# Gate projections of a hybrid decoder block: weight sums without a negation, one of four made by an accumulating load

## The chip, the cores and the metric

The kernel runs on one core of a Trainium2 chip. The metric is the device time of one execution in microseconds (us). The kernel before took 425.77 us in the median of three runs (425.74 to 426.47). Durations below come from one further execution that was recorded by the hardware profiler.

The core has a matrix engine (TensorE, "PE" in the profile), a vector engine (VectorE, "DVE"), an activation engine (ScalarE, "ACT"), a general engine (GpSimd, "POOL") and a queue engine that only issues transfers (SyncE, "SP"). TensorE writes its results to PSUM banks. ScalarE, GpSimd and SP issue transfers (DMAs). Every engine works through its own queue of instructions in order and waits on semaphores for the others.

## The reference

The input x has 512 rows and 1024 columns. It is normalised, multiplied with one wide weight matrix, and the product is cut into the inputs of two attention branches and of two gates:

```
h = rms_norm(x, norm_g);  proj = h @ w_in
fq, fk, fv, fz, mq, mk, mv, mz, ga, gb, fl = split_cols(proj, IN_SPLITS)
y_fox  = fox_attention(...)  * silu(fz)      # 8 heads of 64, with a forget gate
y_moba = moba_attention(...) * silu(mz)      # 8 heads of 64, block-sparse
merged = sigmoid(ga + b_gate[0]) * (y_fox @ w_fox) + sigmoid(gb + b_gate[1]) * (y_moba @ w_moba)
x = x + merged @ w_out
```

The change concerns `ga` and `gb`: two products of h (512 x 1024) with a 1024 x 1024 slice of `w_in` each, followed by a bias and a sigmoid.

## The kernel before

All numbers are float32. Each matmul operand is split into a high part and the rest (`hi` and `lo`), and a product is made of three matmuls: high by high, low by high, high by low. A weight block of 128 x 1024 elements is split by one ScalarE instruction (line 141, `hi`) and one VectorE subtraction (line 143, `lo`). There are four buffers each for `hi` and `lo` and four (`wr`) for raw weights.

The work is staged: loads, normalisation and the first projections; four attention groups (fox a, fox b, moba a, moba b) with the remaining projections laid between their steps; the gates; the output projection. The gates come in four groups, GA0, GA1, GB0 and GB1. Between GB0 and GB1, and after GB1, stand the output products of the moba branch (`wm0` to `wm3`).

Each gate group computes 256 columns out of each half of its gate with a Strassen–Winograd scheme: the activations are cut into blocks A11, A12, A21, A22 (halves of the rows and of the 1024 columns of h), the weights into W11, W12, W21, W22, and seven products take the place of eight. Four of the seven use sums of activation blocks, S1 to S4, and four use sums of weight blocks, T1 to T4.

The activation sums are made once, in `make_sums`, during the first attention group: for each of four pairs of h blocks four VectorE instructions of 128 x 256 elements (line 274), then a split; the parts go to DRAM, and GpSimd's queue loads them back as the gates begin (line 291, eight transfers of 512 KB).

In each group, `group` has

- four loads of 512 KB on SP's queue (line 728), in the order W11, W12, W22, W21;
- seven preparations (`prep`). Each splits one block or sum; ahead of the second, fourth and sixth stand subtractions of 128 x 1024 elements on VectorE (line 723), four in all;
- seven products (`product`, lines 759, 761 and 762) of 24 matmuls each, 256 columns wide, in the order of `PRODUCTS`: A11, S3, A12, S2, S1, A22, S4. They accumulate in three PSUM banks;
- after each product an `evac` step: ScalarE keeps a bank's partial result in SBUF (line 769), or VectorE adds a kept one to a bank (line 772); `finish` applies the sigmoid on ScalarE (lines 802, 804, 805).

`pump` orders loads and preparations around the products: ahead of a unit of TensorE work it queues preparations up to three ahead of it, and a load as soon as the preparation that last reads the buffer it will take has been queued. Each load carries the number of its block's last preparation for that. A planner then sets the order in each engine's queue from its own estimates of durations, under the dependencies of the data.

GpSimd's queue holds, in the moba groups, powers and products for the norms (lines 343, 345), the products of line 670, then the loads of line 291, and, beside the first gate group, two instructions that spread the last head pair's reciprocal row sums (line 663). TensorE transposes those (line 666). In the output stage it issues accumulating loads (`minus`, line 897): ScalarE negates a weight block in place and GpSimd's transfer adds another one from DRAM to it.

Of the kernel before, what the change touches and what calls it, by code (L numbers as in the profile page):

```python
# [9 lines left out]
AF = mybir.ActivationFunctionType  # L10
OP = mybir.AluOpType
# [3 lines left out]
S = 512  # L15
# [4 lines left out]
CW = 256  # L20
# [9 lines left out]
def fox_moba_kernel(ctx: ExitStack, tc, xT, x, w_in, w_fl, w_fox, w_moba, w_out, cst, rope, out):  # L30


    nc = tc.nc
    V, A, G, T = nc.vector, nc.scalar, nc.gpsimd, nc.tensor
# [14 lines left out]
    def t2(tag, bufs, name, shape=(P, 512), dt=F32):  # L49
        pool = stage["pool"] if tag in ("qs", "pt", "pc", "ys") else sb  # L50
        return pool.tile(list(shape), dt, name=name, tag=tag, bufs=bufs)

    def pst(tag, bufs, name):
        return ps.tile([P, 512], F32, name=name, tag=tag, bufs=bufs)
# [36 lines left out]
    def col(c, n=1):  # L91
        return cs[:, c:c + n]
# [45 lines left out]
    def split(src, n, name, half=False):  # L138
        hi = sb.tile([P, 4, 264], F32R, name=f"wh_{name}", tag="wh", bufs=4)
        lo = sb.tile([P, 4, 264], F32R, name=f"wl_{name}", tag="wl", bufs=4)  # L140
        A.activation(hi[:, :, 0:n], src, AF.Copy)  # L141
        for eng, q in ((V, slice(0, 2)), (G, slice(2, 4))) if half else ((V, slice(0, 4)),):
            eng.tensor_tensor(out=lo[:, q, 0:n], in0=src[:, q], in1=hi[:, q, 0:n].bitcast(F32), op=OP.subtract)  # L143
        return hi, lo
# [27 lines left out]
    COLS = {}  # L172
# [87 lines left out]
    HT = S // 2  # L260
# [4 lines left out]
    def make_sums(k):  # L265
        def tl(tag, dt=F32):
            return t2("y", 15, f"sum_{tag}", dt=dt)
        a, b = XT[k], XT[k + 4]
        out = []
        f0, f1 = tl("sf"), tl("sf")  # L270
        s3, s2, s1, s4 = f0[:, 0:HT], f0[:, HT:S], f1[:, 0:HT], f1[:, HT:S]
        for o, x, y, op in ((s3, a[:, 0:HT], a[:, HT:S], OP.subtract), (s1, a[:, HT:S], b[:, HT:S], OP.add),
                            (s2, s1, a[:, 0:HT], OP.subtract), (s4, b[:, 0:HT], s2, OP.subtract)):
            V.tensor_tensor(out=o, in0=x, in1=y, op=op)
        for i, f in enumerate((f0, f1)):
            hl = [tl("sh", F32R), tl("sl", F32R)]
            A.activation(hl[0], f, AF.Copy)
            V.tensor_tensor(out=hl[1], in0=f, in1=hl[0].bitcast(F32), op=OP.subtract)
            out.extend((d[2 * i:2 * i + 2, :, k, :].rearrange("s p t -> p s t"),
                        t.bitcast(F32).rearrange("p (s t) -> p s t", t=HT)) for d, t in zip(S_dram, hl))  # L280

        def store():
            for d, t in out:
                A.dma_start(out=d, in_=t)
        return store
# [7 lines left out]
    def left(what, k):  # L293
        if what[0] == "S":
            return [x[:, k] for x in SB[S_AT[what]]]
        t, kk = int(what[1]) - 1, 4 * (int(what[2]) - 1) + k
        return [x[:, kk, t * HT:(t + 1) * HT] for x in (Gh, Gl)]
# [411 lines left out]

    PRODUCTS = (("A11", 1), ("S3", 3), ("A12", 2), ("S2", 1), ("S1", 1), ("A22", 3), ("S4", 1))
    groups = {}

    def group(name):
        ga, i = name[1] == "A", int(name[2])
        wa, wb = (f"g{'a' if ga else 'b'}{i}", f"g{'a' if ga else 'b'}{i + 2}")
        st = {}
        R, B = {}, {}
        base = len(preps)  # L720

        def sub(o, a, b):
            V.tensor_tensor(out=o, in0=a, in1=b, op=OP.subtract)

        def load(key, nm, hf):
            def go():
                R[key] = sb.tile([P, 4, CW], F32, name=f"wr_{nm}{hf}", tag="wr", bufs=WR)
                nc.sync.dma_start(out=R[key], in_=w_in[COLS[nm] // CW, :, 4 * hf:4 * hf + 4, :])
            return go

        def prep(n):

            def go():
                if n == 1:
                    sub(R["11"], R["12"], R["11"])
                    sub(R["12"], R["22"], R["12"])
                elif n == 3:
                    sub(R["12"], R["22"], R["11"])
                elif n == 5:
                    sub(R["21"], R["21"], R["12"])  # L740
                key = ("11", "12", "21", "12", "11", "21", "22")[n]
                B[n] = split(R[key], CW, f"{name}{n}")
            return go
        for key, nm, hf, last in (("11", wa, 0, 4), ("12", wb, 0, 5), ("22", wb, 1, 6), ("21", wa, 1, 5)):
            loads.append((load(key, nm, hf), base + last))
        preps.extend(prep(n) for n in range(7))

        def product(n):
            what, b = PRODUCTS[n]
            if n < 3:  # L750
                st[b] = pst(("pj", "tp", "tp")[b - 1], (2, 3, 3)[b - 1], f"pb{b}_{name}")
            p = st[b]
            hi, lo = B[n]
            for c in range(2):
                o = p[:, c * HT:(c + 1) * HT]
                cc = slice(c * P, (c + 1) * P)
                for k in range(4):
                    lh, ll = left(what, k)
                    T.matmul(o, hi[:, k, cc], lh, start=(n < 3 and c == 0 and k == 0), stop=False,  # L759
                             skip_group_check=True)  # L760
                    T.matmul(o, hi[:, k, cc], ll, start=False, stop=False, skip_group_check=True)  # L761
                    T.matmul(o, lo[:, k, cc], lh, start=False, stop=(k == 3), skip_group_check=True)  # L762

        def two(a):
            return a.rearrange("p (c t) -> p c t", t=HT)

        def keep(n, b):
            st["e", n] = stage["pool"].tile([P, S], F32, name=f"e{n}_{name}", tag="e", bufs=3)
            A.activation(st["e", n], st[b], AF.Copy)

        def add(u, half, n, b):
            V.tensor_tensor(out=u[:, :, half * HT:(half + 1) * HT], in0=two(st[b]), in1=two(st["e", n]), op=OP.add)

        def evac(n):
            if n == 0:
                if ga or i == 0:
                    u = [sb.tile([P, 2, S], F32, name=f"u{name}{q}", tag="qk", bufs=4) for q in range(2)]
                else:
                    v4 = sb.tile([P, 4, S], F32, name=f"u{name}", tag="v", bufs=2)
                    u = [v4[:, 0:2, :], v4[:, 2:4, :]]  # L780
                st["u"] = u
                keep(1, 1)
            elif n == 1:
                keep(3, 3)
            elif n == 2:
                add(st["u"][0], 0, 1, 2)
            elif n == 3:
                keep(2, 1)
            elif n == 4:
                add(st["u"][1], 1, 3, 1)  # L790
            elif n == 5:
                add(st["u"][0], 1, 2, 3)
                finish(0)
            else:
                finish(1)

        def finish(q):
            u, j0 = st["u"][q], 2 * i + 4 * q
            bg = C_BG + (0 if ga else 8)
            for c in range(2):  # L800
                if q == 0:
                    A.activation(u[:, c, :], u[:, c, :], AF.Sigmoid, bias=col(bg + j0 + c))
                else:
                    A.activation(u[:, c, 0:HT], two(st[1])[:, c, :], AF.Sigmoid, bias=col(bg + j0 + c))
                    A.activation(u[:, c, HT:S], u[:, c, HT:S], AF.Sigmoid, bias=col(bg + j0 + c))
            if ga:
                f = FS[j0 // 2]
                V.tensor_tensor(out=f, in0=u, in1=f, op=OP.mult)
            else:
                SG[j0 // 2] = u  # L810

        def unit(n):
            def go():
                product(n)
                evac(n)
            return go
        groups[name] = [unit(n) for n in range(7)]
# [295 lines left out]
    prep, product, evac, sub, result = (groups[k] for k in ("prep", "product", "evac", "sub", "out"))  # L1113
# [115 lines left out]
```

## Time and profile before

| what | value |
|---|---|
| median of the runs | 425.77 us (425.74 to 426.47) |
| the profiled execution | 425.43 us |
| its span on the core | 423.4 us |
| TensorE matmuls, busy | 417.7 us |
| VectorE, busy | 326.8 us |
| ScalarE, busy | 269.5 us |
| GpSimd, busy | 106.3 us |
| moved by DMA | 58.21 MB |

The span runs from the first to the last record of the core; 425.43 - 423.4 = 2.0 us lie around it. In the profile's rows, a group shows line, engine, operation, output and inputs, count, then busy time in us and mean duration in ns, and after the last bar the idle time of the engine before these instructions with what ended it. A timeline row shows start and duration in us. "L723" is line 723 of the kernel. The row of a line or a tile shows the shortest, median and longest duration in ns and the first and last start.

### The profile page before, as it was taken

The numbers are of one execution on the slowest core, as the hardware profiler recorded it, in microseconds if no ns is written. First come the engines' busy times: TensorE is split into PE (matmuls) and PEld (weight loads), VectorE is DVE, ScalarE is ACT, GpSimd is POOL, SyncE is SP. The second block draws the span as 40 slices with busy tenths as digits, with TensorE's granted clock in tenths as the row PEclk, the third lists the DMA queues.
The fourth block names the chain that finished last, engine by engine and source line by source line (L and its number), as shares of the span: only waits on it lengthen the run. The fifth ranks groups of instructions, "written<-read, shape, count | busy, mean of one in ns | idle before, by whom it ended". The sixth has DMA issues, their size and how long they took to land.

```text
span 423.4 us, 7713 instructions
## 1 busy us (share of the span) xinstructions
PE 417.7 (99%) x2913; PEld 388.9 (92%) x2913; DVE 326.8 (77%) x570; ACT 269.5 (64%) x515; POOL 106.3 (25%) x120
## 2 busy tenths in 40 slices
PE   8999999999999999999999999999999999999996
PEld 6998899999999998899998888899999989988885
DVE  4679977899967768578676787767979698689883
ACT  4986327778767767567656686756656535686450
POOL 1065730225136550016660202140000000022330
PEclk9999999999999999999999999999999999999999
DMA  7973334666263323314123222473042603696484
GB/s 242 396 257 112 100 101 127 183 198 211 77 209 108 100 78 125 82 45 124 31 96 114 88 74 82 154 279 110 31 170 66 233 2 121 206 253 116 100 142 157
DMA packets 25621, 58.21 MB, mean 137 GB/s; under 512 B 3064, under 2 KB 7856, under 8 KB 25584
## 3 DMA queue, kind: packets, MB, share of 16 engines
q1 hardware_dynamic: 13392, 38.11, 27.7%
q10 hardware_dynamic: 8800, 11.21, 8.7%
q0 software_dynamic: 3392, 8.39, 8.5%
q8 instruction: 23, 0.38, 0.3%
q14 instruction: 14, 0.11, 0.1%
HBM read 48.11 MB, written 6.32 MB: 129 GB/s over the span
## 4 chain that ended last, share of the span: by engine, by line
PE 97%; DMA 1%; SPq 0%; DVE 0%; issue 0%; ACT 0%
PE pb_GB L762 3%; PE pb_GA L762 3%; PE pb_GB L759 3%; PE pb_GA L759 3%; PE pb_GB L761 3%; PE pb_GA L761 3%; PE po L950 3%; PE po L949 3%; PE po L948 3%; PE lg L565 2%; PE pv L620 2%; PE pv L619 2%; PE lg L564 2%; PE pf L690 2%; PE pf L689 2%; PE pm L690 2%
## 5 line engine op out<-in xcount | busy, mean ns | idle before, releaser
L343 POOL TENSOR_TENSOR ff<-ss,mh 128x8 f32<-128x8 f32 x16 | 32.0, 2005 | 71.0 <-DVE ss L341 63.2
L567 DVE CUSTOM_DVE_ANT_0 p<-lg,mask 128x128 f32<-128x128 f32 (+1 forms) x64 | 30.6, 488 | 15.7 <-PE lg L565 15.3
L569 ACT ACTIVATE p<-p,negm 128x128 f32<-128x128 f32 (+1 forms) x64 | 35.6, 557 | 10.0 <-DVE negm L567 9.7
L897 POOL DMA_DIRECT2D wr_o<-in_w_out_dram x4 | 4.9, 1293 | 95.4 <-DMA wr_o<-in_w_out_dram 87.2
L143 DVE TENSOR_TENSOR wl_GA<-wr_ga,wh_GA 128x1024 fp32r<-128x1024 f32 x14 | 16.9, 1223 | 7.6 <-ACT wh_GA L141 5.8
L141 ACT ACTIVATE wh_GA<-wr_ga 128x1024 fp32r<-128x1024 f32 x14 | 14.6, 1059 | 9.9 <-PE pb_GA L761 4.9
L141 ACT ACTIVATE wh_GB<-wr_gb 128x1024 fp32r<-128x1024 f32 x14 | 14.6, 1059 | 9.5 <-PE pm L689 3.5
L564 PE MATMUL lg<-KH,QS 128*128 128x128 f32 (+1 forms) x64 | 20.3, 327 | 0.0
L910 ACT ACTIVATE wh_o<-wr_o 128x1024 fp32r<-128x1024 f32 x14 | 14.8, 1060 | 8.2 <-PE pb_GB L761 2.8
L911 DVE TENSOR_TENSOR wl_o<-wr_o,wh_o 128x1024 fp32r<-128x1024 f32 x14 | 17.0, 1221 | 3.8 <-ACT wh_o L910 3.8
L143 DVE TENSOR_TENSOR wl_GB<-wr_gb,wh_GB 128x1024 fp32r<-128x1024 f32 x14 | 16.9, 1222 | 3.5 <-ACT wh_GB L141 3.5
L645 DVE TENSOR_TENSOR ypair<-pv,ysh 64x512 f32<-64x512 f32 x16 | 11.0, 687 | 5.8 <-ACT ysh L644 5.5
L337 DVE TENSOR_REDUCE ss<-sq 128x8 f32<-128x512 f32 x16 | 10.9, 679 | 4.6 <-ACT sq L336 4.5
L538 DVE SCALAR_TENSOR_TENSOR QS<-p_qT,cs,QS 64x512 fp32r<-64x512 f32 x16 | 12.0, 750 | 2.4 <-ACT QS L537 2.0
L759 PE MATMUL pb_GA<-Gh,wh_GA 128*128 128x256 f32 x48 | 13.6, 282 | 0.0
L761 PE MATMUL pb_GA<-Gl,wh_GA 128*128 128x256 f32 x48 | 13.5, 281 | 0.0
L762 PE MATMUL pb_GA<-Gh,wl_GA 128*128 128x256 f32 x48 | 13.5, 281 | 0.0
L762 PE MATMUL pb_GB<-Gh,wl_GB 128*128 128x256 f32 x48 | 13.5, 281 | 0.0
L761 PE MATMUL pb_GB<-Gl,wh_GB 128*128 128x256 f32 x48 | 13.4, 281 | 0.0
L759 PE MATMUL pb_GB<-Gh,wh_GB 128*128 128x256 f32 x48 | 13.3, 281 | 0.0
L542 DVE SCALAR_TENSOR_TENSOR KL<-p_kT,cs,KH 64x512 fp32r<-64x512 f32 x16 | 12.0, 749 | 1.3 <-ACT KH L540 0.8
L537 ACT ACTIVATE QS<-p_qT,cs 64x512 fp32r<-64x512 f32 x16 | 10.9, 680 | 3.3 <-DVE QS L538 2.2
(459 smaller groups left out, 1792.8 us busy)
## 6 DMA issues: line engine op xcount, KB each, us to landing
wr_ga<-in_w_in_dram SPq DMA_DIRECT2D x8, 512.0 KB
wr_gb<-in_w_in_dram SPq DMA_DIRECT2D x8, 512.0 KB, 5.1
wr_o<-in_w_out_dram SPq DMA_DIRECT2D x8, 512.0 KB, 12.6
xt<-in_xT_dram SPq DMA_DIRECT2D x8, 256.0 KB, 6.9
x<-in_x_dram SPq DMA_DIRECT2D x8, 256.0 KB, 6.0
KH<-KH ACTq DMA_DIRECT2D x16, 128.0 KB, 4.8
s_dramh<-sum_sh ACTq DMA_DIRECT2D x8, 256.0 KB, 5.5
s_draml<-sum_sl ACTq DMA_DIRECT2D x8, 256.0 KB, 2.5
```

The costliest lines, as they stand in the source:

```text
L141: A.activation(hi[:, :, 0:n], src, AF.Copy)
L143: eng.tensor_tensor(out=lo[:, q, 0:n], in0=src[:, q], in1=hi[:, q, 0:n].bitcast(F32), op=OP.subtract)
L343: G.tensor_tensor(out=f2, in0=ss.rearrange("p t h -> p (t h)"), in1=mh, op=OP.pow)
L564: T.matmul(lg[:, :n], qs[:, qt], kh[:, :n], start=True, stop=False)
L567: V.tensor_tensor_reduce(pt, lg[:, :n], mask[:, 512 - n:512], -0.125, 3.0e38, op0=OP.add, op1=OP.min, accum_out=mkn[:, hh, i:i + 1])
L569: A.activation(pt, pt, AF.Exp, bias=mkn[:, hh, i:i + 1], scale=-1.0, accum_out=rs[:, hh, i:i + 1])
L690: T.matmul(p, lo[:, k, cc], yh, start=False, stop=(k == 3))
L759: T.matmul(o, hi[:, k, cc], lh, start=(n < 3 and c == 0 and k == 0), stop=False, skip_group_check=True)
L761: T.matmul(o, hi[:, k, cc], ll, start=False, stop=False, skip_group_check=True)
L762: T.matmul(o, lo[:, k, cc], lh, start=False, stop=(k == 3), skip_group_check=True)
L910: A.activation(wide(hi), wide(R[key, c]), AF.Copy)
L911: V.tensor_tensor(out=wide(lo), in0=wide(R[key, c]), in1=wide(hi).bitcast(F32), op=OP.subtract)
```

## The change

The signs of the activation sums are chosen so that each weight sum is a chain of additions and one subtraction in place, and the block that enters first, W12 + W22, is made while loading.

- `make_sums`: S1 is now A22 - A21; S2 and S4 are made with a multiplication by -1 and a subtraction in one instruction. There are still four instructions of 128 x 256 for each of the four pairs.
- Loads of a group: W12, W11, W21, W22 on SP's queue. Behind W12, GpSimd's queue loads W22 with addition into the same tile, so W22 is read from DRAM twice.
- Preparations: the fourth adds W12 + W22 to W11; the fifth adds W11's tile to W21's and subtracts W22 from W11's. That is three VectorE instructions a group where there were four.
- Order of the products: A11, A12, S3, S2, S1, A22, S4. The steps after the second and third product change places with them.
- The second column's result comes out negated, and the sigmoids of `finish(1)` take a scale of -1. (`finish(0)` is as it was.)

```diff
@@ make_sums
-        for o, x, y, op in ((s3, a[:, 0:HT], a[:, HT:S], OP.subtract), (s1, a[:, HT:S], b[:, HT:S], OP.add),
-                            (s2, s1, a[:, 0:HT], OP.subtract), (s4, b[:, 0:HT], s2, OP.subtract)):
-            V.tensor_tensor(out=o, in0=x, in1=y, op=op)
+        V.tensor_tensor(out=s3, in0=a[:, 0:HT], in1=a[:, HT:S], op=OP.subtract)
+        V.tensor_tensor(out=s1, in0=b[:, HT:S], in1=a[:, HT:S], op=OP.subtract)
+        V.scalar_tensor_tensor(s2, s1, -1.0, a[:, 0:HT], op0=OP.mult, op1=OP.subtract)
+        V.scalar_tensor_tensor(s4, s2, -1.0, b[:, 0:HT], op0=OP.mult, op1=OP.subtract)
@@ PRODUCTS
-    PRODUCTS = (("A11", 1), ("S3", 3), ("A12", 2), ("S2", 1), ("S1", 1), ("A22", 3), ("S4", 1))
+    PRODUCTS = (("A11", 1), ("A12", 2), ("S3", 3), ("S2", 1), ("S1", 1), ("A22", 3), ("S4", 1))
@@ group
-        def sub(o, a, b):
-            V.tensor_tensor(out=o, in0=a, in1=b, op=OP.subtract)
+        def plus(o, a, b, op=OP.add):
+            V.tensor_tensor(out=o, in0=a, in1=b, op=op)
+
+        def rows(nm, hf):
+            return w_in[COLS[nm] // CW, :, 4 * hf:4 * hf + 4, :]
...
-                nc.sync.dma_start(out=R[key], in_=w_in[COLS[nm] // CW, :, 4 * hf:4 * hf + 4, :])
+                nc.sync.dma_start(out=R[key], in_=rows(nm, hf))
+                if key == "12":
+                    G.dma_start(out=R[key], in_=rows(wb, 1), accum_op=OP.add)
...
-                if n == 1:
-                    sub(R["11"], R["12"], R["11"])
-                    sub(R["12"], R["22"], R["12"])
-                elif n == 3:
-                    sub(R["12"], R["22"], R["11"])
-                elif n == 5:
-                    sub(R["21"], R["21"], R["12"])
-                key = ("11", "12", "21", "12", "11", "21", "22")[n]
+                if n == 3:
+                    plus(R["11"], R["11"], R["12"])
+                elif n == 4:
+                    plus(R["21"], R["21"], R["11"])
+                    plus(R["11"], R["11"], R["22"], OP.subtract)
+                key = ("11", "21", "12", "11", "11", "21", "22")[n]
...
-        for key, nm, hf, last in (("11", wa, 0, 4), ("12", wb, 0, 5), ("22", wb, 1, 6), ("21", wa, 1, 5)):
+        for key, nm, hf, last in (("12", wb, 0, 3), ("11", wa, 0, 4), ("21", wa, 1, 5), ("22", wb, 1, 6)):
@@ evac: n == 1 and n == 2 change places
@@ finish
-                    A.activation(u[:, c, 0:HT], two(st[1])[:, c, :], AF.Sigmoid, bias=col(bg + j0 + c))
-                    A.activation(u[:, c, HT:S], u[:, c, HT:S], AF.Sigmoid, bias=col(bg + j0 + c))
+                    A.activation(u[:, c, 0:HT], two(st[1])[:, c, :], AF.Sigmoid, bias=col(bg + j0 + c), scale=-1.0)
+                    A.activation(u[:, c, HT:S], u[:, c, HT:S], AF.Sigmoid, bias=col(bg + j0 + c), scale=-1.0)
```

More of the change, by code (lines that the diff above doesn't have):

```diff
@@ L783, in evac @@
             elif n == 1:
+                add(st["u"][0], 0, 1, 2)
+            elif n == 2:
                 keep(3, 3)
-            elif n == 2:
-                add(st["u"][0], 0, 1, 2)
             elif n == 3:
```

## The prediction

> **What bounds the kernel now.** I read the page's busy shares, its forty slices and its chain first, then the list of waits of the TensorE queue, then the stretches of the gate stage, and last the end of the timeline.
>
> ```profile
> PE 417.7 (99%) x2913; PEld 388.9 (92%) x2913; DVE 326.8 (77%) x570; ACT 269.5 (64%) x515; POOL 106.3 (25%) x120
> PE   8999999999999999999999999999999999999996
> PE 97%; DMA 1%; SPq 0%; DVE 0%; issue 0%; ACT 0%
> ```
> ```profile
> PE warm_ps L107 <- DVE fg_pre L480: 1.5, 1, 1.5
> PE fqa L392 <- DVE wl_fqa L168: 0.5, 1, 0.5
> ```
> ```profile
> 419.52 0.28 PE L950 MATMUL po<-wh_o,mg 128*128 128x256 f32 x1
> ...
> 419.85 0.42 DVE L970 TENSOR_TENSOR ot<-po,eo 128x256 f32<-128x256 f32 x1 [0.88 <-PE po L950]
> ...
> 420.30 0.36 SPq L972 DMA_DIRECT2D out_dram<-ot  x1
> ```
> ```profile
> 276.70:296.00 19.30, 19.30 (x163) 19.21 (x162) 13.50 (x18) 10.93 (x16) 4.29 (x5) 1.00 0.57 193
> 296.00:312.50 16.50, 16.50 (x142) 16.50 (x141) 14.39 (x14) 10.07 (x15) 0.00 (x0) 1.00 0.35 118
> 312.50:332.00 19.50, 19.50 (x167) 19.50 (x166) 16.66 (x16) 11.53 (x16) 0.00 (x0) 1.00 0.32 111
> 332.00:346.00 14.00, 14.00 (x89) 12.53 (x88) 10.71 (x13) 7.46 (x11) 0.00 (x0) 1.00 0.25 86
> 346.00:370.00 24.00, 24.00 (x178) 22.79 (x177) 18.07 (x22) 12.86 (x18) 0.00 (x0) 1.00 0.43 137
> ```
>
> The columns of the last fence are length, TensorE, weight loads, VectorE, ScalarE, GpSimd, granted clock, DMA share, GB/s. 97% of the chain that ended last is TensorE. In the whole trace its queue waits for another engine twice, 2.0 us together, both at the start and untouched by the change. Through the four gate groups (276.7 to 370) it is busy in every microsecond, at clock 1.00. VectorE is busy 13.50/19.30 = 70% to 16.66/19.50 = 85% there. The end is a fixed tail: last matmul at 419.52, its addition at 419.85, the last store issued at 420.30, end at 423.4. So the time is the start, TensorE's own work and the tail. An edit that takes work from VectorE shortens none of the three; one that makes a weight block late lengthens the second.
>
> **The change part by part.**
>
> ```profile
> L723 DVE TENSOR_TENSOR wr_ga<-wr_ga,wr_ga 128x1024 f32<-128x1024 f32 x8 | 9.8, 1222 | 0.1
> L723 DVE TENSOR_TENSOR wr_gb<-wr_gb,wr_gb 128x1024 f32<-128x1024 f32 x8 | 9.7, 1218 | 0.1
> L143 DVE TENSOR_TENSOR wl_GB<-wr_gb,wh_GB 128x1024 fp32r<-128x1024 f32 x14 | 16.9, 1222 | 3.5 <-ACT wh_GB L141 3.5
> L831 DVE TENSOR_TENSOR uGB<-pm,uGB 128x512 f32<-128x512 f32 x5 | 3.4, 689 | 1.0 <-PE pm L690 0.8
> L434 DVE SCALAR_TENSOR_TENSOR zs_mzb<-sg,pz_mzb 128x512 f32<-128x512 f32 x2 | 1.4, 682 | 1.8 <-ACT sg L433 1.8
> L538 DVE SCALAR_TENSOR_TENSOR QS<-p_qT,cs,QS 64x512 fp32r<-64x512 f32 x2 | 1.5, 750 | 0.1
> L141 ACT ACTIVATE wh_GB<-wr_gb 128x1024 fp32r<-128x1024 f32 x14 | 14.6, 1059 | 9.5 <-PE pm L689 3.5
> L802 ACT ACTIVATE uGA<-uGA,cs 128x512 f32<-128x512 f32 x4 | 2.7, 717 | 4.0 <-DVE uGA L772 4.0
> ```
> ```profile
> L274 DVE TENSOR_TENSOR sum_sf<-sum_sf,xt x4: 406/424/426, 70.1 to 111.9; 128x256 f32<-128x256 f32 x4
> ```
> ```profile
> 262.94 0.73 ACT L569 ACTIVATE p<-p,negm 128x512 f32<-128x512 f32 x1
> ```
>
> *Activation sums.* Eight of the sixteen additions of 128x256 (424 ns) become a multiply-and-subtract with the constant -1. A multiply-and-add with a constant took 682 ns at 128x512 (L434), the plain multiplication of one PSUM and one SBUF operand of that shape 689 ns (L831): no difference. With a per-partition scalar it was 750 ns (L538), 61 ns over L831. The bounds are 0 and 8 x 0.061 = 0.5 us of VectorE; I take 0, since the new scalar is a constant as in L434. The cover is TensorE's full queue.
>
> *Weight sums.* Sixteen subtractions of 1.22 us (19.5 us) become twelve additions or subtractions (14.6 us): 4.9 us off VectorE, 1.2 us a group. TensorE waited for none of them, so the gain in time is 0, and VectorE idles longer.
>
> *Sigmoid with scale -1.* The exponential of 128x512 with a scale of -1 and a bias took 0.73 us (L569), the sigmoid with the default scale 0.72 us (L802). 0. Swapping the second and third product moves 24 equal matmuls past 24 others. 0.
>
> *The accumulating load.* Each group reads W22 a second time, 512 KB on GpSimd's queue, which first waits for the plain load of W12 into the same tile, and the third split waits for the sum.
>
> ```profile
> wr_gb<-in_w_in_dram SPq DMA_DIRECT2D x8, 512.0 KB, 5.1
> ...
> S3h<-s_dramh POOLq DMA_DIRECT2D x1, 512.0 KB, 6.6
> ```
> ```profile
> L897 POOL DMA_DIRECT2D wr_o<-in_w_out_dram x4: 1194/1244/1491, 370.8 to 382.4; - x4
> ...
> DMA to landing us min/median/max: 6.7/7.9/9.9
> ```
> ```profile
> 276.90 12.41 SPq L728 DMA_DIRECT2D wr_ga<-in_w_in_dram  x4
> 304.72 4.99 SPq L728 DMA_DIRECT2D wr_gb<-in_w_in_dram  x4
> 326.93 8.39 SPq L728 DMA_DIRECT2D wr_gb<-in_w_in_dram  x4
> ```
> ```profile
> 297.67 2.35 DVE L143 TENSOR_TENSOR wl_GA<-wr_ga,wh_GA 128x1024 fp32r<-128x1024 f32 x2
> 299.94 2.48 DVE L723 TENSOR_TENSOR wr_ga<-wr_ga,wr_ga 128x1024 f32<-128x1024 f32 x2
> ```
> ```profile
> L759 PE MATMUL pb_GB<-S0h,wh_GB x16: 277/282/287, 321.2 to 351.9; 128*128 128x256 f32 x16
> ```
> ```profile
> 301.20 0.28 PE L759 MATMUL pb_GA<-S0h,wh_GA 128*128 128x256 f32 x1
> ...
> 324.03 0.28 PE L759 MATMUL pb_GB<-Gh,wh_GB 128*128 128x256 f32 x1
> ...
> 352.25 0.40 PE L759 MATMUL pb_GB<-Gh,wh_GB 128*128 128x256 f32 x2
> ```
>
> The same kind of load, accumulating and 512 KB, stands in the output stage (L897): 1.24 us of GpSimd, 6.7 to 9.9 us from issue to landing. The tightest group is GB0, straight behind GA1. In the new order the W12 tile is the first that GA1 gives up: after its third split (the second of the two L143 at 297.67, over at 300.0) and one 1.22 us addition, so about 301.2. Its next load is then issued at 301.2; the worst I allow is 304.7, where the first GB0 load is issued now. Plain landing (5.1 us): 306.3 to 309.8. Accumulating landing: 306.3 + 6.7 = 313.0 at best, 309.8 + 9.9 = 319.7 at worst. The split (1.06 us on ScalarE, L141, then 1.22 us on VectorE, L143, together 2.3 us) ends at 315.3 to 322.0. The second product of GB0 now begins at 321.2 and the third at 324.03 (24 matmuls in 2.83 us, 0.118 us each), and the swap leaves the third place where it is. Slack 8.7 to 2.0 us: no stall.
>
> GA1 and GB1 have more. GA1's tile is loaded at 276.9 at the latest; with 6.6 us for a load among the sum loads (S3h) and 9.9 us it is complete at 293.4 and split at 295.7, needed one product behind the second one (301.20 + 24 x 0.118 = 304.0). GB1: 326.9 + 5.1 + 9.9 + 2.3 = 344.2, needed at 352.25. GA0 is loaded long before.
>
> What is queued behind the new wait on GpSimd:
>
> ```profile
> 238.55 2.26 POOL L670 TENSOR_TENSOR rinv_bc<-zs_mza,rinv_bc 128x512 f32<-128x512 f32 x1 [17.85 <-DMA rinv_bc<-r_dram]
> ...
> 280.85 2.68 POOL L663 TENSOR_SCALAR rinv_w<-rinv 128x256 f32<-128x256 f32 x2
> ```
> ```profile
> 288.94 0.49 PE L666 MATMUL p_rinv<-ident,rinv_w 128*128 128x128 f32 x3
> ```
>
> For GA0 it falls into the 17.85 us idle stretch ahead of 238.55. For GA1 it falls among the sum loads, and the reciprocal rows at 280.85 may stand behind it; TensorE reads them at 288.94, 288.94 - 283.53 = 5.4 us after they are ready. For GB0 and GB1 GpSimd has nothing (0.00 busy from 296 to 370). SP's queue keeps its four loads a group, with W12 first and W11 second instead of first. For GB0 that is 4.99/3 = 1.7 us later than 304.7 if the four are evenly spaced: landed at 311.5, split at 313.8. GB0's first product runs one product of GA1 and its own ahead of 321.2, at 315.5, so 1.7 us are left. DMA carries 4 x 0.5 = 2 MB more where it is 25% to 57% busy.
>
> The sum: 0 + 0 + 0 + 0. The profiled execution took 425.43 us (span 423.4), 0.34 us under the median of the runs, 425.77; with no difference I predict that median, 425.8.
>
> [...]
>
> [...]
>
> **The rivals.**
>
> *Slower: the W12 sum arrives late.* A third place in the queue, not the first, would issue GB0's load near 309 (the end of the row at 304.72): 309 + 5.1 + 9.9 + 2.3 = 326.3, 2.3 us past 324.03. It decides from an issue at 324.0 - 17.3 = 306.7 on. For it: the planner places the wait by its own estimate of this load, and engines work in order. Against it: W12 is released first. Time 425.8 + 2.3 = 428.1.
>
> *Slower: the reciprocal rows are held up.* If GA1's W12 load lands later than 288.94 - 2.68 - 1.24 = 285.0 and stands ahead of L663, TensorE stops. Issued at 276.9 and landing in 9.9 us it would: 286.8 against 285.0, 1.8 us, 427.6. Against it: 6.6 us is the slowest plain row there, 283.5.
>
> [...]
>
> *Faster: TensorE does have room.* If the gapless row hides waiting for VectorE, at most the 4.9 us come back: 420.9. Against it: the 0.118 us a matmul in a product that no engine holds up, and weight loads that fill the same stretches. A new order by the planner, which sees other costs, could also shift the tail from 419.52 to 423.4; I estimate a quarter of these 3.9 us, 1 us, either way: 424.8 or 426.8.
>
> **How the numbers follow.** Runs of this kernel spread over 0.17% (425.74 to 426.47), so 0.2% (0.85 us) is about the least to be told from nothing. No change 0.62. Late sum 0.13, reciprocal rows 0.04, descriptors 0.03, worse order 0.05: slower 0.25. Better order 0.10, room on TensorE 0.03: faster 0.13. The likeliest case alone spans 424.9 to 426.6; up to 428.2 it takes in the late sum and the rows held up, and down to 424.6 the better order: about 0.85 of the chance.
>
> **What would show it.** Right: twelve additions of 1.22 us instead of sixteen, VectorE near 322 us busy, four accumulating loads of 512 KB from GpSimd with 7 to 10 us to landing, no new wait in TensorE's list. Wrong: TensorE waiting for ScalarE or VectorE at a third product, or for L663's rows, or a TensorE total that differs from 417.7 us by more than 0.5 us.

## The result, and the profile after

The changed kernel took 427.82 us in the median of seven runs (427.12 to 430.21), the kernel before 425.74 us (425.33 to 426.47) on the same chip. The ratio is 1.0056, with a 95% interval of 1.0033 to 1.0080: slower by 2.1 us. The time lies inside the range given, but the case called likeliest, no difference, did not happen. The profiled execution took 427.31 us, 1.88 us more than that of before.

The page of the changed kernel (busy us, share, instructions), and its list of waits of the TensorE queue:

```profile
span 425.2 us, 7715 instructions
PE 417.5 (98%) x2913; PEld 387.9 (91%) x2913; DVE 322.6 (76%) x566; ACT 269.8 (63%) x515; POOL 107.9 (25%) x124
PE   7999999999999999999999999999989999999996
```
```profile
PE warm_ps L107 <- DVE fg_pre L481: 1.5, 1, 1.5
PE fqa L392 <- ACT Zh L131: 1.1, 1, 1.1
PE pb_GB L765 <- ACT wh_GB L141: 1.1, 1, 1.1
PE fqa L393 <- DVE wl_fqa L168: 0.4, 1, 0.4
```

TensorE's own work is the same (417.5 against 417.7 us), and VectorE has 4.2 us less. One wait is new: GB0's first matmul waits for ScalarE's split of its weights. The waits named `fqa` and `warm_ps` lie in the first 11 us and were there in other forms before. They are 1.0 us longer together, but TensorE is only 0.06 us later than before as it reaches GB0, so they are not the loss. TensorE at the same place in the kernel before, then around the new wait (start and duration in us):

```profile
312.59 0.28 PE L759 MATMUL pb_GB<-Gh,wh_GB 128*128 128x256 f32 x1
312.71 0.28 PE L761 MATMUL pb_GB<-Gl,wh_GB 128*128 128x256 f32 x1
```
```profile
312.54 0.28 PE L768 MATMUL pb_GA<-Gh,wl_GA 128*128 128x256 f32 x1
313.90 0.38 PE L765 MATMUL pb_GB<-Gh,wh_GB 128*128 128x256 f32 x1 [1.08 <-ACT wh_GB L141]
314.13 0.28 PE L767 MATMUL pb_GB<-Gl,wh_GB 128*128 128x256 f32 x1
314.39 0.39 PE L765 MATMUL pb_GA<-S2h,wh_GA 128*128 128x256 f32 x1
314.61 0.28 PE L767 MATMUL pb_GA<-S2l,wh_GA 128*128 128x256 f32 x1
...
421.30 0.28 PE L956 MATMUL po<-wh_o,mg 128*128 128x256 f32 x1
```

In both kernels TensorE runs two matmuls of GB0's first product ahead of a product of GA1. In the changed one, from 312.54 to 314.61, four steps take 2.07 us where four steps of 0.118 us would take 0.47: 1.60 us are lost here. The last matmul starts at 421.30, 1.78 us later than before. So nine tenths of this execution's loss lie at one place. What led to it, from the queues of SP, GpSimd and ScalarE in turn:

```profile
300.32 0.33 SPq L734 DMA_DIRECT2D wr_gb<-in_w_in_dram  x1
306.26 1.47 SPq L734 DMA_DIRECT2D wr_gb<-in_w_in_dram  x2
```
```profile
304.38 0.93 POOL L736 DMA_DIRECT2D wr_gb<-in_w_in_dram  x1 [19.52 <-DMA wr_gb<-in_w_in_dram]
...
334.43 0.88 POOL L736 DMA_DIRECT2D wr_gb<-in_w_in_dram  x1 [29.12 <-DMA wr_gb<-in_w_in_dram]
```
```profile
307.10 1.06 ACT L141 ACTIVATE wh_GA<-wr_ga 128x1024 fp32r<-128x1024 f32 x1 [1.79 <-PE pb_GA L767]
308.06 0.58 ACT L775 ACTIVATE e_GA<-pb_GA 128x512 f32<-128x512 f32 x1
312.79 1.06 ACT L141 ACTIVATE wh_GB<-wr_gb 128x1024 fp32r<-128x1024 f32 x1 [4.15 <-PE pb_GA L767]
313.76 0.58 ACT L775 ACTIVATE e_GA<-pb_GA 128x512 f32<-128x512 f32 x1
```

W12 of GB0 is issued at 300.32, and the accumulating load of W22 follows at 304.38. W11 is issued at 306.26, when the second tile comes free, and its split on ScalarE starts at 312.79, 6.5 us later. (The row names TensorE as the last to release it. But the trace's semaphore records have this load complete at 312.69, 0.1 us before the split; and in the run without GB0's accumulating load, below, the same split starts over 2 us before the TensorE product that is named here ends. So it is the load.) Behind the split, in the same queue, stands `e_GA`, the copy of a PSUM bank to which GA1's next product adds.

A second wait on a sum, on VectorE, does not reach TensorE in this execution. It lies in GB1, whose accumulating load was issued at 334.43:

```profile
341.73 1.23 DVE L726 TENSOR_TENSOR wr_gb<-wr_gb,wr_gb 128x1024 f32<-128x1024 f32 x1 [1.03 <-DMA wr_gb<-in_w_in_dram]
342.87 0.69 DVE L838 TENSOR_TENSOR uGB<-uGB,f 128x512 f32<-128x512 f32 x1
```

### The profile page after: what moved, and what is told of

It is laid out like the page before. It is cut to its first block, busy times and chain, and to the rows that moved or that the text cites. A ratio compares the mean times of both kernels' runs of the same rounds, so it can differ in the third digit from the quotient of the medians.

```text
span 425.2 us, 7715 instructions
## 1 busy us (share of the span) xinstructions
PE 417.5 (98%) x2913; PEld 387.9 (91%) x2913; DVE 322.6 (76%) x566; ACT 269.8 (63%) x515; POOL 107.9 (25%) x124
## 3 DMA queue, kind: packets, MB, share of 16 engines
q0 software_dynamic: 3968, 10.49, 11.7%
## 4 chain that ended last, share of the span: by engine, by line
PE 96%; DMA 1%; SPq 0%; ACT 0%; DVE 0%; issue 0%; ACTq 0%
PE pb_GB L765 3%; PE pb_GA L765 3%; PE pb_GB L768 3%; PE pb_GA L767 3%; PE pb_GB L767 3%; PE pb_GA L768 3%; PE po L956 3%; PE po L955 3%; PE po L954 3%; PE pv L621 2%; PE lg L566 2%; PE pv L620 2%; PE lg L565 2%; PE pm L689 2%; PE pf L691 2%; PE pm L690 2%
## 5 line engine op out<-in xcount | busy, mean ns | idle before, releaser
L645 ACT ACTIVATE ysh<-pv 64x512 f32<-64x512 f32 x16 | 9.5, 594 | 7.6 <-PE pv L621 7.1
L736 POOL DMA_DIRECT2D wr_gb<-in_w_in_dram x2 | 1.8, 906 | 48.6 <-DMA wr_gb<-in_w_in_dram 48.6
```

## The experiments

All are compared with runs of the kernel before on the same chip. A run that leaves out a load or a subtraction leaves out that part of the result. The first four were meant to tell apart theory A (the new load order and two early matmuls in TensorE's queue), theory B (the accumulating load slows W11's load beside it) and theory C (a spread loss). The rest follow from what they showed.

| run | median us | ratio to before, 95% interval |
|---|---|---|
| changed kernel again | 427.58 | 1.0046, 1.0029 to 1.0063 |
| GB0's first product pinned behind GA1's | 429.22 | 1.0098, 1.0069 to 1.0127 |
| W11 loaded first | 432.92 | 1.0162, 1.0139 to 1.0186 |
| no accumulating load in GB0 | 426.28 | 1.0016, 1.0006 to 1.0025 |
| none in GB1 | 426.78 | 1.0028, 1.0020 to 1.0037 |
| none in GB0 and GB1 | 425.27 | 0.9991, 0.9983 to 0.9999 |
| plain second load, not added | 426.52 | 1.0023, 1.0009 to 1.0037 |
| VectorE's sum in GB0 | 430.07 | 1.0084, 1.0060 to 1.0109 |
| signs alone, VectorE's sum everywhere | 426.75 | 1.0026, 1.0013 to 1.0038 |
| the same with the old load order | 429.00 | 1.0083, 1.0064 to 1.0103 |
| before with three subtractions a group | 425.68 | 1.0002, 0.9992 to 1.0013 |
| W11 loaded first, once more (2 runs) | 433.84 | 1.0193, 1.0168 to 1.0217 |

**The changed kernel once more.** No edit.

> The changed kernel once more, for its spread and for a second look at the stall. Theory A (W11 of GB0 is now the second load of its group and comes late, and TensorE meets two of its matmuls at 312.5 already): 427 to 429 us again, with a wait of TensorE for ScalarE's first split of GB0 of 1 to 3 us that accounts for most of the difference to before. Theory C (the loss is spread over many places, or lies in the run and not in the kernel): the time or the place of the wait differs from one execution to the next, and the wait at GB0 is not there every time.

427.58 us. TensorE waits at the same matmul for the same split, 1.0 us:

```profile
PE pb_GB L765 <- ACT wh_GB L141: 1.0, 1, 1.0
...
PE pm L689 <- ACT uGB L810: 0.2, 1, 0.2
```

The place is the same in both profiles, so theory C falls for most of the loss. A small second wait is at a moba product (`pm`), behind GB1's sum.

**GB0's first product pinned.**

```diff
-                product(n)
+                if name == "GB0" and n == 0:
+                    with behind(mybir.EngineType.PE):
+                        product(n)
+                else:
+                    product(n)
```

> The changed kernel with one constraint: GB0's first product stands behind all of GA1's products traced before it in TensorE's queue, so the two early matmuls are gone from in front of GA1's S1 product; loads, sums and splits are untouched. Theory A: W11 is then first needed one product (2.8 us) later, near 315.4, and is split by 314 to 315: no wait, 425.7 to 426.2 us. Theory B (the accumulating read beside it slows W11's load) alone gives the same here. Theory C: 427.3 us or more, as before this constraint.

429.22 us, slower still. The two early matmuls are gone, and the wait has moved to the product that now comes next:

```profile
315.19 0.38 PE L765 MATMUL pb_GA<-S2h,wh_GA 128*128 128x256 f32 x1 [1.87 <-ACT e_GA L775]
```
```profile
313.60 1.06 ACT L141 ACTIVATE wh_GB<-wr_gb 128x1024 fp32r<-128x1024 f32 x1 [4.45 <-DMA wr_gb<-in_w_in_dram]
314.56 0.58 ACT L775 ACTIVATE e_GA<-pb_GA 128x512 f32<-128x512 f32 x1
```

GA1's S1 product adds to the bank that `e_GA` copies, and so has to wait for it. `e_GA` could have run about 3 us earlier (without GB0's accumulating load, below, it ran at 311.45), but is queued behind the split that waits for W11's load; here the row names the DMA. So the two early matmuls are not the cause. My half of theory A about the two early matmuls falls: the 4.45 us that the split waited for the late load held up `e_GA` behind it in ScalarE's queue.

**W11 loaded first.**

```diff
-        for key, nm, hf, last in (("12", wb, 0, 3), ("11", wa, 0, 4), ("21", wa, 1, 5), ("22", wb, 1, 6)):
+        for key, nm, hf, last in (("11", wa, 0, 4), ("12", wb, 0, 3), ("21", wa, 1, 5), ("22", wb, 1, 6)):
```

> The changed kernel with the loads in the order W11, W12 (with its accumulating load), W21, W22. Theory A: W11 of GB0 is issued near 300.3 instead of 306.3 and lands by 307; no wait at GB0's first matmuls. The sum W12 + W22 comes later: issued 306.3, landed 312, accumulated by 319.5, split by 322, against a need near 325: 425.7 to 426.2 us. The rival that I forecast (the sum arrives late) would show here: a wait at GB0's third product of up to 2 us, 427 to 428 us. Theory C: 427.3 us or more.

432.92 us. The wait at GB0's first matmul is gone, as theory A and B both say, but two larger ones take its place. TensorE's list, then GpSimd's and VectorE's rows in GB0:

```profile
PE pb_GB L765 <- ACT wh_GB L141: 2.6, 1, 2.6
PE pb_GB L768 <- DVE wl_GB L143: 1.6, 1, 1.6
```
```profile
310.42 0.88 POOL L736 DMA_DIRECT2D wr_gb<-in_w_in_dram  x1 [22.89 <-DMA wr_gb<-in_w_in_dram]
```
```profile
317.80 1.23 DVE L726 TENSOR_TENSOR wr_gb<-wr_gb,wr_gb 128x1024 f32<-128x1024 f32 x1 [4.34 <-DMA wr_gb<-in_w_in_dram]
318.95 1.22 DVE L143 TENSOR_TENSOR wl_GB<-wr_gb,wh_GB 128x1024 fp32r<-128x1024 f32 x1
```

The sum of GB0 now lands at 317.7, inside the 319.5 that I allowed. But the addition of W12's sum to W11's tile stands early in VectorE's queue, and the split of the second product behind it waits 4.3 us with it: TensorE's wait of 1.6 us. The wait of 2.6 us is at GB1's first product, where the same addition waits 4.2 us for GB1's sum. This is the rival of the prediction (the sum arrives late), at an earlier consumer than I had named. With the accumulating load, either order of the two loads puts one of them too late.

**No accumulating load in GB0.**

```diff
-                if key == "12":
+                if key == "12" and name != "GB0":
```

> The changed kernel without the accumulating load in group GB0 alone (W22 is not added to W12 there, so that part of the result is left out of the computation); the order of TensorE's queue around GB0's start is the same, with the two early matmuls. If the load order alone does it (A without B), W11 is issued at 306.3 and lands as late as now, near 312.7: the wait stays at 1.1 us or more, 427 us. If the accumulating read lengthens W11's landing (B), the landing shrinks from 6.5 to about 5.1 us, the first split is over near 312.6 and the wait falls to 0.3 us or less: 425.9 to 426.3 us.

426.28 us, 1.3 us less than the changed kernel. W11 is issued at 306.65 and its split starts at 310.48, 3.8 us later instead of 6.5 (the load itself took at most those 3.8 us here, and 6.4 us by the semaphore records of the changed kernel); nothing waits at GB0's start:

```profile
310.48 1.06 ACT L141 ACTIVATE wh_GB<-wr_gb 128x1024 fp32r<-128x1024 f32 x1 [1.45 <-PE pb_GA L768]
```

The same stretch in the kernel before, the changed kernel and here (last columns: clock, DMA share, GB/s):

```profile
306.30:309.00 2.70, 2.70 (x25) 2.70 (x24) 2.23 (x3) 1.06 (x1) 0.00 (x0) 1.00 0.82 256
```
```profile
306.30:309.00 2.70, 2.70 (x25) 2.70 (x25) 1.88 (x2) 1.55 (x2) 0.00 (x0) 1.00 0.87 168
```
```profile
306.30:309.00 2.70, 2.70 (x25) 2.70 (x24) 1.87 (x3) 1.51 (x2) 0.00 (x0) 1.00 0.48 118
```

With the accumulating load the DMA engines are 87% busy at 168 GB/s, without it 48% at 118. (In the kernel before three loads of the group are under way here, and engines that are 82% busy move 256 GB/s.) Theory B holds for GB0.

**A plain second load.**

```diff
-                    G.dma_start(out=R[key], in_=rows(wb, 1), accum_op=OP.add)
+                    G.dma_start(out=R[key], in_=rows(wb, 1))
```

> The changed kernel with GpSimd's second load written plainly over W12's tile instead of added to it (T3 and what is built on it leave W12 out); same queue, same size, same waits, and the same order of TensorE's queue around GB0's start. If any 512 KB beside W11's load delays it (B2), the first split of GB0 starts near 312.7 as now and TensorE waits about 1 us: 427.2 to 428 us. If it is the addition, which costs the DMA engines more time for a byte (B1: the share of GpSimd's queue rose from 8.5% to 11.7% for 2.1 MB, 1.5% a MB, against 0.73% a MB on SP's queue), W11 lands about 1.5 us sooner and the wait is 0.3 us or less: 425.9 to 426.5 us.

426.52 us, just above the range for B1, and the profile shows B1: W11's split starts at 310.87 after an issue at 306.05, 4.8 us, and TensorE has no wait in the gates.

```profile
310.87 1.06 ACT L141 ACTIVATE wh_GB<-wr_gb 128x1024 fp32r<-128x1024 f32 x1 [2.44 <-DMA wr_gb<-in_w_in_dram]
```

But the profiled execution, 425.38 us, was the fastest of twelve, so what the others lose to the kernel before (0.9 us in the median, up to 428.9 us) has no profile. The software queue of GpSimd on the page, in the changed kernel and here:

```profile
q0 software_dynamic: 3968, 10.49, 11.7%
```
```profile
q0 software_dynamic: 3968, 10.49, 10.2%
```

The 2.1 MB more cost 11.7 - 8.5 = 3.2 points of the DMA engines' time when they are added and 10.2 - 8.5 = 1.7 points when copied (8.5% was the queue's share before). Here an accumulating byte cost about twice a copied one. A copy beside W11 was not free either: 4.8 us against at most 3.8 without it.

**VectorE's sum in GB0.**

```diff
-                if key == "12":
+                if key == "12" and name != "GB0":
...
+                if n == 2 and name == "GB0":
+                    plus(R["12"], R["12"], R["22"])
```

> The changed kernel with W12 + W22 made by a VectorE addition in group GB0 alone, the other three groups with the accumulating load. Theory B: no wait at GB0's start, 425.9 to 426.4 us, as without the sum. Rival: W22, the last load of the group (issued near 309.4, landed 314.5, added 315.8, split by 318.1), now has to be there for the third split; if the first splits and evacuations stand behind it in their queues, TensorE waits again: 427 us or more.

430.07 us: the second expectation, and in another group. GB0 has no wait; in GB1, whose sum was issued later (336.32), TensorE waits 2.0 us. What follows the wait cost nearly as much again (an estimate: 0.46 of 3.7 us is 1.7 us):

```profile
PE pb_GB L767 <- ACT wh_GB L141: 2.0, 1, 2.0
```
```profile
344.80:347.20 2.40, 0.44 (x3) 0.06 (x1) 1.40 (x4) 1.47 (x3) 0.00 (x0) 1.00 0.00 0
347.20:350.90 3.70, 3.58 (x9) 2.71 (x10) 3.70 (x5) 1.75 (x4) 0.00 (x0) 0.54 0.02 4
350.90:355.00 4.10, 4.10 (x24) 3.53 (x23) 2.87 (x5) 0.86 (x2) 0.00 (x0) 1.00 0.42 128
```

After 2.4 almost empty microseconds the granted clock (the column behind GpSimd's) is 0.54 for 3.7 us. The three executions above 430 us have a granted clock of 0.994 to 0.996 over the whole span, the other three 1.00.

**Signs alone.** No accumulating load; in every group VectorE adds W22 to W12 ahead of the third split.

```diff
-                if key == "12":
-                    G.dma_start(out=R[key], in_=rows(wb, 1), accum_op=OP.add)
...
+                if n == 2:
+                    plus(R["12"], R["12"], R["22"])
```

> The changed kernel without any accumulating load: signs, order of loads and products as changed, and W12 + W22 made by a VectorE addition in every group (four VectorE instructions a group, as before the change). If the accumulating loads are the whole loss: 425.2 to 425.9 us, no difference to before. If the load order or the signs cost something by themselves: 426.2 us or more, with a wait of TensorE in a gate group.

426.75 us: not the same as before. The first case fails, and the second's number comes: the accumulating loads are not the whole price of making this sum. The new wait is TensorE's at a moba product, 0.8 us for VectorE, which itself waits for W22, the last load of GB1:

```profile
PE pm L689 <- DVE uGB L837: 0.8, 1, 0.8
```
```profile
340.29 1.23 DVE L726 TENSOR_TENSOR wr_gb<-wr_gb,wr_gb 128x1024 f32<-128x1024 f32 x1 [1.16 <-DMA wr_gb<-in_w_in_dram]
341.43 0.68 DVE L837 TENSOR_TENSOR uGB<-pm,uGB 128x512 f32<-128x512 f32 x1
```

**Before with three subtractions a group.** The kernel before without its fourth subtraction.

```diff
-                elif n == 5:
-                    sub(R["21"], R["21"], R["12"])
```

> The kernel before without the fourth subtraction of each group (the sixth preparation splits W21 instead of W21 less a sum, so that part is left out of the computation). 4.9 us less on VectorE. My step: worth nothing, 425.1 to 425.8 us. Rival (TensorE's gapless row hides waits for VectorE): up to 4.9 us less, 420.5 to 424.5 us.

425.68 us, ratio 1.0002. VectorE's relief is worth nothing; the rival that TensorE has hidden room falls.

**No accumulating load in GB1.**

```diff
-                if key == "12":
+                if key == "12" and name != "GB1":
```

> The changed kernel without the accumulating load in group GB1 alone (W22 is not added to W12 there, so that part of the computation is left out). In the changed kernel VectorE waits 1.0 us at 341.7 for that sum, with the evacuation of a moba product behind it. Theory D (the wait on a late sum is paid by what stands behind it in VectorE's and ScalarE's queues): the wait at GB0's start stays, 1.0 to 1.4 us, and the slow executions (429 us and more) go: 426.9 to 427.5 us in the median. If GB1's sum costs nothing: 427.6 us or more, as the changed kernel.

426.78 us (426.28 to 427.75), 0.8 to 1.0 us less than the changed kernel, and no execution above 428 us. TensorE still waits for GB0's first split, though 0.5 us in this profile, less than expected:

```profile
PE pb_GB L765 <- ACT wh_GB L141: 0.5, 1, 0.5
```

Theory D holds in the main: GB1's load has a price of its own. The edit takes away both the wait for the sum and the traffic of its load; which of them counts was not separated.

**None in GB0 and GB1.**

```diff
-                if key == "12":
+                if key == "12" and ga:
```

> The changed kernel without the accumulating load in GB0 and GB1 (left out of the computation there); GA0 and GA1 keep it. If the loss is these two loads and nothing else: 425.4 to 425.9 us, no wait of TensorE in the gates. If signs, load order or the loads of GA0 and GA1 cost something too: 426.2 us or more, with a wait in the trace that names it.

425.27 us (424.90 to 425.70), ratio 0.9991: the whole loss is gone, and TensorE's list has only the start:

```profile
PE warm_ps L107 <- DVE fg_pre L481: 1.5, 1, 1.5
PE fqa L393 <- DVE wl_fqa L168: 0.6, 1, 0.6
```

The signs, the order of loads and products and the accumulating loads of GA0 and GA1 cost nothing together, as long as no sum W12 + W22 is made in GB0 and GB1. The loss is the two loads there: alone they were worth 1.3 to 1.5 and 0.8 to 1.0 us, together 2.3 to 2.6.

**Signs alone with the old load order.**

```diff
-        for key, nm, hf, last in (("12", wb, 0, 3), ("11", wa, 0, 4), ("21", wa, 1, 5), ("22", wb, 1, 6)):
+        for key, nm, hf, last in (("11", wa, 0, 4), ("12", wb, 0, 3), ("22", wb, 1, 6), ("21", wa, 1, 5)):
```

(and the edit of the signs alone)

> The new signs and the new order of products, but no accumulating load, W12 + W22 made by VectorE, and the loads in the order of the kernel before (W11, W12, W22, W21). If the signs are free and the 0.26% of the run with signs alone came from W22 standing last in the queue: 425.3 to 425.9 us and no wait in the gates. If the signs or the order of products cost something: 426.2 us or more.

429.00 us, more than with the new load order: the first case fails, and moving W22 up does not help. Of GB0's loads only W11 is issued early here, at 304.2; W12, W22 and W21 follow from 309.4 to 311.7. W12 + W22 needs both tiles, and VectorE waits for it with the second split's work behind it:

```profile
316.54 1.23 DVE L726 TENSOR_TENSOR wr_gb<-wr_gb,wr_gb 128x1024 f32<-128x1024 f32 x1 [3.51 <-DMA wr_gb<-in_w_in_dram]
```

TensorE waits 1.2 us in GB0 and 1.6 us in GB1. So with these signs the sum W12 + W22 can be late by VectorE too. In the kernel before, whose second preparation already reads W22, the first three loads of GB0 are issued within 2.3 us from 304.7 on. Which load order would serve the new signs was not tried further.

**W11 loaded first, once more.** No edit to that run.

> The run with W11 loaded first once more, for a second profile of its long wait (2.6 us at GB1's first product). In the run with VectorE's sum in GB0 a wait of 2.0 us was followed by 3.7 us at half the TensorE clock. If a long wait itself brings the clock down, some executions of this kernel show a granted clock under 1.00 and times above 432 us; a profile that catches one shows matmul steps of 0.43 instead of 0.23 us behind the wait. If the clock is not tied to the wait: 1.00 throughout.

433.64 and 434.05 us. TensorE's wait at GB1's first product is 2.7 us, and behind it the clock comes down:

```profile
346.00:349.00 3.00, 1.11 (x5) 0.56 (x3) 1.95 (x3) 0.57 (x2) 0.00 (x0) 1.00 0.00 0
349.00:353.00 4.00, 2.93 (x9) 2.22 (x10) 3.48 (x5) 2.47 (x4) 0.00 (x0) 0.75 0.01 4
353.00:357.00 4.00, 4.00 (x21) 3.46 (x20) 3.15 (x5) 0.48 (x2) 0.00 (x0) 0.82 0.32 108
```

From 351.2 to 354.2 the steps between its 128x512 matmuls are 0.43 us instead of 0.23. In the first profile of the same kernel, at 430.58 us, a wait of 2.6 us had no such drop, and that execution's granted clock was 1.00; the other four of that run, 432.07 us and more, list 0.992 to 0.996, the two here 0.996. In GB0 this profile has a wait of 2.4 us, at 321.51, and the 128x256 matmuls behind it keep their step of 0.12 us. So of the four waits of 2.0 to 2.7 us in these three profiles, two (2.0 and 2.7 us) were followed by about 3 us at steps of 0.43 us, and two (2.4 and 2.6 us) were not.

## Why the prediction was right or wrong

*What bounds the kernel, and the gains: right.* TensorE's work stayed, VectorE fell to 322.6 us, and the run with three subtractions shows that this is worth nothing. The two instructions with a constant -1 took 421 and 411 ns in the mean, those in their place before 420 and 409 ns.

*The accumulating load's own duration: right, with a margin.* 5.4 to 7.2 us to landing, where I took 6.7 to 9.9. No third product waited for its sum in the changed kernel.

*SP's queue, "so 1.7 us are left" for W11 of GB0: wrong, and it carries the larger part.* The issue was right (306.26; my even spacing gives 306.4). The landing was not: I took 5.1 us, from a load with no accumulating transfer beside it. With GB0's accumulating load issued 1.9 us earlier it took up to 6.5 us, without it at most 3.8. And the need was not at 315.5. The trace of before has two matmuls of GB0's first product at 312.59 and 312.71; and ScalarE's queue holds GA1's `e_GA` behind the split, which the product right after them has to wait for. I had counted whole products back from TensorE's next reading and not asked what stands behind the instruction that waits for it. The 1.7 us were not there: with my own 311.5 for the landing ScalarE's part of the split ends at 312.6, just in time, and the longer landing then became TensorE's wait.

*"GB1: 344.2, needed at 352.25": wrong in the need.* The sum was there at 341.7, earlier than I allowed, but VectorE's addition in the fourth preparation, which reads it, stands ahead of the evacuation of a moba product. Taking GB1's load away gave 0.8 to 1.0 us; the two profiles of the changed kernel show little of it (0.2 us at a moba product in one).

*DMA "25% to 57% busy", so 2 MB more are hidden: wrong as a reading.* In the stretch that counted, 306.3 to 309, they were 87% busy, and 82% in the kernel before, whose mean over 296 to 312.5 is 35%.

*The rivals.* The late sum, priced at 2.3 us (428.1) for GB0's third product, came in GB1 and through VectorE's queue, where it cost 0.8 to 1.0 us. The larger part is W11 of GB0, which had no rival and no price. So that the measured 427.82 lies inside the range and near 428.1 is luck: the range reached up to 428.2 for other causes. The reciprocal rows were not held up: TensorE's list has no wait for them. No run shows the term "descriptors 0.03": GpSimd issued its accumulating loads in 0.88 to 1.06 us, the one at 304.38 in 0.93 us while VectorE was busy throughout. TensorE's room and the better order did not show. The chance of 0.25 for slower was too small: the estimate of 0.62 rested on slack measured against TensorE alone.

*What stays open.* How the loss of the slowest executions of the changed kernel (429.3 and 430.2 us) is made up has no profile. A longer wait in GB1 fits both. The clock drop of the two runs above fits the second, whose granted clock is 0.996 over the span, but not the first, which lists 1.00. Either is argued and not shown.

## What to carry to other kernels

The new wait here cost what stood behind the waiting instruction in its own engine's queue (with GB0's first product pinned, 1.87 us at `e_GA`), so slack had to be taken to the first such neighbour that the bound engine needs, not to the reader of the data. Where a transfer is added beside loads that are just in time, take their landing from a stretch with the same traffic: an accumulating transfer here took about twice the DMA time of a copy (3.2 against 1.7 points for 2.1 MB) and put the split of its neighbour's block 2.7 us later (6.5 against 3.8 us after the issue). Relief on an engine that the bound engine never waits for was worth nothing here (a ratio of 1.0002 with three subtractions a group), and did not pay for that.

## What the runs showed of the hardware that was not expected

A byte added by DMA took the DMA engines about twice as long as a copied one (3.2 against 1.7 points of their time for 2.1 MB).

After a TensorE wait of 2.0 us the granted clock fell to 0.54 over 3.7 us, and after one of 2.7 us to 0.75 and 0.82 over 4 us each; so the wait of 2.0 us cost nearly as much again (an estimate: 0.46 of 3.7 us is 1.7 us). Waits of 2.4 and 2.6 us had no such drop behind them. What decides between the two was not shown.
